# Experts' sums stored to their tokens' rows and read back in order; the last three experts added by products

## The chip, the core and the metric

The kernel runs on one core of one Trainium2 chip. The metric is the device time of one execution in microseconds (us). The core has a matrix engine (PE), a vector engine (VectorE, DVE), a scalar engine (ScalarE, ACT), GpSimd (POOL) and a queue that only issues transfers (SyncE, SP); 16 DMA engines carry the transfers of all queues. In the profile's DMA section q1 carries what SP issues, q10 what ScalarE issues, q0 what POOL issues.

## The reference

Two layers over 256 tokens `x` and 256 context tokens, each of width 1024. Layer 0 updates all 512 rows, layer 1 only the 256 of `x`. Each layer has a normalized, modulated attention and mixing part and then a mixture of 16 experts, of which each token uses two:

```python
h = rmsnorm(x, g) * (1 + scale) + shift
top2, weight = route(h)                    # grouped top-2 of 16 experts
for e in 16 experts:                       # d_model 1024 -> 512 -> 1024
    y[e] = (silu(h @ wg[e]) * (h @ wu[e])) @ wd[e]
x = x + gate * (weight[0] * y[top2[0]] + weight[1] * y[top2[1]])
out = rmsnorm(x, final_g)                  # after layer 1, rows of x only
```

All products of the experts are float32; each expert has 6 MB of weights a layer.

## The kernel before

**Slots.** An expert works on slots: 96 for the first `WIDE` experts of a layer (10 in layer 0, 6 in layer 1), 64 for the rest, which are taken in order of load. `g_route` writes a table `tab` of six numbers per token and expert (token number and weight, in pieces). A one-hot product with it gives each slot's token number `ids` and weight `csl`; an empty slot gets a number past the end, so its row is not gathered. `turn_tokens(e)` turns an expert's gathered rows for PE, `widen` makes the two projections, `inner` and `turn_inner` the gating, and `down` or `down_narrow` the third product and the scaled sums `yo`.

**Weights.** `Stream` (`W`) holds the list of all weight tiles in the order of use. `W.ahead()` issues loads on SP as far as free buffers and `W.limit` allow, several experts ahead. PE's order is written by hand; in the loop over `e` of `moe`, expert `e`'s projections stand between the parts of expert `e-1`.

**Sums and their way back.** `yo` of every expert goes, empty slots too, to `ybuf`, a buffer in DRAM laid out by expert and slot, by plain stores on ScalarE's queue (L1310, L1334). `rest()`, some 28 small VectorE instructions after expert 1, works out for each token the two rows `rowi` at which its sums stand. `combine_get` (L1182) gathers them by indirect loads on POOL, `combine` adds the two (L1190), multiplies by the gate in layer 0 (L1192) and adds to the token's row `xs` (L1194).

**The tail.** The last `TAIL` experts (two in layer 0, one in layer 1) reach the rows of `x` without DRAM: `others` keeps the scaled sums in `yx` (L1399), a product with a one-hot matrix `hotT` puts them at their tokens (`others_add`, L1366), and VectorE adds the product to `xs` (L1406). The gathers of the `x` rows are issued before the last expert's product in layer 0 and behind it in layer 1. Half of one tile's combine is done on POOL.

**After the experts.** In layer 0 the context's 256 rows are gathered (`yg`, `yh`), combined by VectorE and POOL, and normalized for layer 1; meanwhile two generators of projections (`uv0`, `uv1`) run, and two more (`ug`) beside the first half of the Hyena mixing (`g_hyf`). In layer 1 follow ScalarE's sums of squares (`junk`, L491), a square root with a table load (L493), VectorE's scaling (L2162) and the store of the output.

Of the kernel before, what the change touches and what calls it, by code (L numbers as in the profile page):

```python
# [36 lines left out]
TAIL = (2, 1)  # L37
# [212 lines left out]
def tile_hybrid_flow(ctx, tc, xin, rows, adab, w_ada, w_in_e, w_out_e, sinkb, rpb, w_in_o, w_out_o, hyw,  # L250
# [40 lines left out]
    def row_at(l, e):  # L291

        return min(e, WIDE[l]) * SLOTS[l] + max(e - WIDE[l], 0) * NARROW

    ybuf = [dram.tile([row_at(l, NE) + 1, D], F32, name=f"ybuf{l}") for l in range(2)]
# [30 lines left out]
    hyn = keep.tile([P, 8], F32, name="hyn")  # L326
    warm = keep.tile([P, 1], F32, name="warm")
# [629 lines left out]
    def slot_table(l, pool):  # L957

        NT = 4 if l == 0 else 2
        tab = pool.tile([P, NT, NE, 6], BF, name=f"tab{l}")  # L960
        tb3 = tok_b.rearrange("p (i a) -> p i a", a=2)[:, 0:NT]
        for a in range(2):
            G.tensor_copy(tab[:, :, :, a], tb3[:, :, a : a + 1].to_broadcast([P, NT, NE]))
        G.tensor_copy(tab[:, :, :, 2:3], cc("far").unsqueeze(1).unsqueeze(2).to_broadcast([P, NT, NE, 1]))
        return tab

    def g_route(l, pool, s, r):
# [78 lines left out]
        ids = kt("ids", [P, NE], I32)  # L1046
        csl = kt("csl", [P, NE])

        def find(src, n, idst, hp):
# [3 lines left out]
            newest["slots"] = V.tensor_scalar_add(idst, f, 4096.0).ins  # L1053

        def weigh(src, cdst):
            V.reduce_sum(cdst, src[:, :, 3:6], axis=AX.X)

        def slots(es, parts, idp=None):
            idp = tpt(f"ids{l}_{es[0]}")[:, 0] if idp is None else idp
            for e in es:  # L1060
                for i in range(NT):
                    hot = one_hot(pool, lambda i: posm[:, i * NE + e : i * NE + e + 1], 0, i, 4, e >= WIDE[l])
                    o = 6 * (e - es[0])
                    T.matmul(idp[:, o + parts.start : o + parts.stop], hot, tab[:, i, e, parts], start=(i == 0), stop=(i == NT - 1))
            return idp[:, 0 : 6 * len(es)].rearrange("p (e a) -> p e a", a=6)
# [37 lines left out]
        comb = rt("comb")  # L1103
# [15 lines left out]
        def group(e, idp):  # L1119

            idp = slots([e], slice(0, 6), idp)
            at = slice(e, e + 1)

            def rest():
                find(idp, 1, ids[:, at], pool)
                weigh(idp, csl[:, at])

            return rest

        def rest():  # L1130
            eb = kt("eb", [P, 2, NT])
# [9 lines left out]
            less = float(C - NARROW)  # L1141
            ri, late = kt("ri", [P, 2, NT]), kt("late", [P, 2, NT])
            V.scalar_tensor_tensor(ri, eb, float(SLOTS[l]), pq, op0=ALU.mult, op1=ALU.add)
            V.tensor_scalar(late, eb, float(-WIDE[l]), 0.0, op0=ALU.add, op1=ALU.max)
            V.scalar_tensor_tensor(ri, late, -less, ri, op0=ALU.mult, op1=ALU.add)
# [3 lines left out]
            rowi = keep.tile([P, 2 * NT], I32, name=f"rowi{l}")  # L1149
            zero = float(row_at(l, NE - TAIL[l]))  # L1150
            V.tensor_scalar(late, eb, NE - TAIL[l] - 0.5, None, op0=ALU.is_gt)
            V.scalar_tensor_tensor(ri, ri, -zero, late, op0=ALU.add, op1=ALU.add)
            V.tensor_mul(ri, ri, inm)
            V.tensor_scalar(late, late, -1.0, 1.0, op0=ALU.mult, op1=ALU.add)
            V.tensor_mul(ri[:, :, NT - 2 :], ri[:, :, NT - 2 :], late[:, :, NT - 2 :])
            V.tensor_scalar_add(rowi, ri.rearrange("p a i -> p (a i)"), zero)
            cmx = rt("cmx", [P, 1])
            top = rt("rtmp")[:, 0:NE]
            V.tensor_scalar(top, place, WIDE[l] - 0.5, less, op0=ALU.is_gt, op1=ALU.mult)
            V.tensor_add(top, top, pos[:, n16:])  # L1160
            V.reduce_max(cmx, top, axis=AX.X)
            cmi = kt("cmi", [P, 1], I32)
            V.tensor_copy(cmi, cmx)
            r.update(eb=eb, pq=pq, inm=inm, ri=ri, rowi=rowi, cmi=cmi)

        yield
        def weigh_first(idp):
            idp = slots([0, 1], slice(3, 6), idp)
            return lambda: weigh(idp, csl[:, 0:2])

        r.update(eids=eids, weigh_first=weigh_first, posm=posm, ids=ids, csl=csl, group=group, rest=rest, find=find, weigh=weigh, one_hot=one_hot, pos=pos)
# [6 lines left out]
    def combine_get(l, ys, src, rows_, i):  # L1178

        NT = 4 if l == 0 else 2  # L1180
        for a, t in enumerate(ys):
            newest["get"] = G.indirect_dma_start(out=t, out_offset=None, in_=src,  # L1182
                                                 in_offset=bass.IndirectOffsetOnAxis(ap=rows_[:, a * NT + i : a * NT + i + 1], axis=0)).ins
        return ys

# [10 lines left out]
    def moe(l, r, gate5):  # L1196
# [5 lines left out]
        posm, tab, ids, csl, one_hot, gts = (r[n] for n in ("posm", "tab", "ids", "csl", "one_hot", "gts"))  # L1202
# [75 lines left out]
        def turn_inner(e, he):  # L1278
# [5 lines left out]
            newest[S] = S.activation(hx[:, 0:2, 0:n], tp[:, 0:2, 0:n], AF.Copy).ins  # L1284
            newest[V] = V.tensor_copy(hx[:, 2:4, 0:n], tp[:, 2:4, 0:n]).ins
            return hx

        def down(e, hx):
# [21 lines left out]
            S.dma_start(yb[e * N : e * N + N, :], yo[0:N])  # L1310

        def down_narrow(e, hx):
# [22 lines left out]
            if l == 0 and e == NE - 1:  # L1335
                W.limit = until_moe0 + 1
                with tc.issue_after(d.ins):
                    W.ahead()
# [3 lines left out]
        def others_slots():  # L1342

            t = W.pools["extra"][0].tile([P, 2, D], F32, name=f"hotT{l}", tag="wt")[:, 0, 0 : 2 * TAIL[l] * P].rearrange("p (n t) -> p n t", t=P)
            tp = tpt(f"hotp{l}")
# [859 lines left out]
```

## Time and profile before

| | |
|---|---|
| median of 3 runs | 1160.65 us (1160.2 to 1163.1) |
| the profiled execution | 1164.05 us |
| its span, first to last instruction | 1162.2 us |
| busy: PE, VectorE, ScalarE, POOL | 1002.1, 557.4, 380.5, 166.0 us |
| moved by DMA | 329.40 MB |
| mean clock granted to PE | 0.94 |

The profiled execution took 1.85 us more than its span and 3.40 us more than the median. Times in the trace count from the first instruction. PE is busy for 86% of the span; the rest is to be looked for stage by stage.

### The profile page before, as it was taken

Reading aid. Unit: us, or ns where it says so; the run is one execution under the profiler, and the core shown is the slowest. Engines: PE = TensorE matmul, PEld = TensorE weight load, DVE = VectorE, ACT = ScalarE, POOL = GpSimd, SP = SyncE. Lnnn points to the kernel's source line nnn. Section 1 sums busy time; section 2 is a strip of 40 time slices with the busy share of each in tenths; the row PEclk is TensorE's granted clock in tenths of the full one; section 3 lists DMA queues with packets and bytes.
Section 4 is the critical chain, followed back from the end, with each engine's and each line's share of the span. In section 5 each row is a group of like instructions: output and inputs, shape, how many; then the busy total and the mean of one; then the engine's idle time right before and its main releaser. Section 6 shows DMA issues by size and latency. Waiting matters only on the chain. (4 is left out here: it accounts for less than half of the span.)

```text
span 1162.2 us, 20926 instructions
## 1 busy us (share of the span) xinstructions
PE 1002.1 (86%) x8390; PEld 554.8 (48%) x8390; DVE 557.4 (48%) x1390; ACT 380.5 (33%) x852; POOL 166.0 (14%) x184
## 2 busy tenths in 40 slices
PE   5899999889893899999998479978884999998881
PEld 2477877557672333333332367766661333332220
DVE  5665555567547533433312874566765533321113
ACT  2554453332322233333221452443341322211111
POOL 2320001210205000000001621312012000000002
PEclk9999999999896899999999789989996999999996
DMA  8931121892967999999999656435297899999993
GB/s 319 417 117 73 73 73 46 297 330 76 393 264 267 312 310 390 403 392 396 403 397 406 252 230 231 154 142 207 73 401 283 278 370 406 408 390 418 418 410 114
DMA packets 56014, 329.40 MB, mean 283 GB/s; under 512 B 8611, under 2 KB 9091, under 8 KB 21795
## 3 DMA queue, kind: packets, MB, share of 16 engines
q1 hardware_dynamic: 40195, 278.85, 61.5%
q0 software_dynamic: 10960, 35.99, 9.3%
q10 hardware_dynamic: 4752, 13.12, 3.2%
q8 instruction: 69, 1.13, 0.4%
q14 instruction: 38, 0.30, 0.1%
HBM read 315.54 MB, written 16.58 MB: 286 GB/s over the span
## 5 line engine op out<-in xcount | busy, mean ns | idle before, releaser
L1234 PE MATMUL gu<-wt,tx 128*32 128x512 f32 x2560 | 305.5, 606 | 12.9 <-DMA wt<-in_moe_wu_dram 10.6
L1234 PEld LDWEIGHTS gu<-wt,tx 128*32 128x32 f32 x2560 | 82.7, 111 | 203.2 <-issue 169.8
L1234 PE MATMUL y<-wt,hx 128*32 128x512 f32 x1280 | 147.5, 593 | 2.4 <-DMA wt<-in_moe_wd_dram 1.5
L1234 PEld LDWEIGHTS y<-wt,hx 128*32 128x32 f32 x1280 | 43.1, 110 | 97.1 <-issue 92.2
L515 DVE TENSOR_TENSOR pair<-wt,pair 128x512 fp32r<-128x512 f32 x104 | 68.8, 711 | 18.5 <-ACT pair L512 18.3
L1223 ACT ACTIVATE tx<-gp 128x192 f32<-128x192 f32 (+1 forms) x64 | 19.3, 304 | 154.7 <-PE gp L1214 119.8
L1265 DVE TENSOR_TENSOR yo<-yo,y 32x512 f32<-32x512 f32 x32 | 21.8, 683 | 90.9 <-ACT yo L1263 90.6
L512 ACT ACTIVATE pair<-wt 128x512 fp32r<-128x512 f32 x104 | 58.4, 626 | 15.6 <-DMA wt<-in_w_in_o_dram 14.5
L1224 DVE COPY tx<-gp 128x192 f32<-128x192 f32 (+1 forms) x64 | 20.3, 322 | 81.5 <-ACT tx L1223 81.0
L1275 DVE TENSOR_TENSOR he<-he,up 96x512 f32<-96x512 f32 (+1 forms) x32 | 21.9, 685 | 72.1 <-ACT up L1274 71.5
L429 PE MATMUL ada<-wt,siluT 128*32 128x128 f32 x1536 | 52.4, 287 | 2.8 <-ACT pt L770 2.0
L1270 ACT ACTIVATE he<-gu 96x512 f32<-96x512 f32 (+1 forms) x32 | 18.9, 591 | 98.8 <-PE gu L1234 98.8
L429 PEld LDWEIGHTS ada<-wt,siluT 128*32 128x32 f32 x1536 | 42.2, 114 | 14.2 <-issue 7.1
L954 POOL DMA_INDIRECT gt<-h2d,ids x16 | 15.5, 972 | 204.5 <-DVE hot L1176 92.2
L954 POOL DMA_INDIRECT rows<-h2d,ids x16 | 15.3, 958 | 185.2 <-DVE hot L1176 95.0
L1265 DVE TENSOR_TENSOR up<-up,gu 32x512 f32<-32x512 f32 x32 | 21.8, 683 | 38.0 <-ACT up L1263 37.7
L768 PE MATMUL tp<-ident,pr 128*128 128x128 f32 x256 | 33.9, 275 | 0.0
L757 DVE TENSOR_SCALAR pr<-pr,ls 128x512 f32<-128x512 f32 (+1 forms) x80 | 32.5, 457 | 1.1
L741 ACT ACTIVATE pr<-sB,ng 128x512 f32<-128x512 f32 (+1 forms) x32 | 18.2, 578 | 41.9 <-DVE ng L734 36.2
L768 PEld LDWEIGHTS tp<-ident,pr 128*128 128x128 f32 x256 | 28.7, 141 | 4.5 <-issue 1.6
L520 PE MATMUL op<-pair,oh 128*128 128x512 f32 x64 | 27.1, 424 | 3.2 <-DVE pair L515 3.1
L519 PE MATMUL op<-pair,ol 128*128 128x512 f32 x64 | 27.7, 433 | 1.7 <-ACT pair L512 1.7
(500 smaller groups left out, 1923.8 us busy)
## 6 DMA issues: line engine op xcount, KB each, us to landing
wt<-in_moe_wg_dram SPq DMA_DIRECT2D x63, 1024.0 KB
wt<-in_moe_wd_dram SPq DMA_DIRECT2D x63, 1024.0 KB
wt<-in_moe_wu_dram SPq DMA_DIRECT2D x62, 1024.0 KB
wt<-in_w_ada_dram SPq DMA_DIRECT2D x45, 1024.0 KB
wt<-in_w_in_e_dram SPq DMA_DIRECT2D x9, 1024.0 KB
ybuf<-yo ACTq DMA_DIRECT2D x16, 384.0 KB
wt<-in_w_in_o_dram SPq DMA_DIRECT2D x5, 1024.0 KB
bc<-mrow POOLq DMA_DIRECT2D x9, 512.0 KB, 10.1
```

The lines of the kernel that those rows point to most:

```text
L429: T.matmul(ps[32 * j : 32 * j + 32, 0:P], siluT[:, k, :], w[:, k % 4, 128 * j : 128 * j + 128], start=(k == 0), stop=(k == KD - 1), tile_p ...
L512: newest["whi"] = S.activation(hi, w, AF.Copy).ins
L515: newest[eng] = eng.tensor_sub(lo, w, hi.bitcast(F32)).ins
L519: T.matmul(o, al, bh, start=first, stop=False)
L520: T.matmul(o, ah, bl, start=False, stop=False)
L757: V.tensor_scalar_mul(pr[:, h, at], pr[:, h, at], ls[:, h, j : j + 1])
L768: T.transpose(tp[:, kc], pr[:, h, kc * P : kc * P + P], ident)
L954: return G.indirect_dma_start(out=dst, out_offset=None, in_=h2d[l], in_offset=bass.IndirectOffsetOnAxis(ap=idx, axis=0), bounds_check=h2d[ ...
L1224: V.tensor_copy(tx[:, q * 4 + 2 : q * 4 + 4, 0:n], tp[:, 2:4, 0:n])
L1234: T.matmul(o[32 * c : 32 * c + 32], lhs, rhs, start=first, stop=last, tile_position=(0, 32 * c))
L1265: V.tensor_add(dst[q : q + 32], dst[q : q + 32], b[q : q + 32])
L1275: V.tensor_mul(he[0:n], he[0:n], up[0:n])
```

## The change

`ybuf` is now laid out by token: two rows for each. `tab` gets a seventh number that tells whether an expert is a token's first or second, and `aim` makes each slot's target row `tgt` from it. `scatter` stores `yo` by an indirect transfer on POOL's queue that skips empty slots; each waits for the one before to land. Since a token's row may not be written when its expert's sum is added by a product or lies past its slots, `ybuf` is first filled with zeros by four transfers from one 1 KB tile (`zero_rows`), 6 MB in pieces of 1 KB. A plain load of 1 MB (`combine_load`) brings 128 tokens' pairs of rows. `TAIL` is three in both layers. `rest()` moves into the branch for overflowing experts; five instructions, `most()`, stay. The last expert's `hx` is copied by ScalarE alone, POOL combines nothing any more, `others_take` runs before the last expert's sums, and layer 1's first weights are issued by SP during expert 15. Behind layer 0 four generators (`u0` to `u3`) stand beside the context's combine. A square root's table is brought in early at the end.

```diff
-TAIL = (2, 1)
+TAIL = (3, 3)
...
-    ybuf = [dram.tile([row_at(l, NE) + 1, D], F32, name=f"ybuf{l}") for l in range(2)]
+    ybuf = [dram.tile([2 * TT, D], F32, name=f"ybuf{l}") for l, TT in enumerate((512, 256))]
...
+        which = rt("sel")
+        V.tensor_scalar(which[:, 0:NE], base, -1.0, 16.0, op0=ALU.mult, op1=ALU.add)
...
+        V.tensor_scalar(which_of, posm, 0.5, None, op0=ALU.is_gt)
+        V.tensor_tensor(i3(which_of), i3(which_of), which[:, 0:NE].unsqueeze(1).to_broadcast([P, NT, NE]), op=ALU.mult)
+        V.reduce_max(first_of, i3(which_of), axis=AX.X)
+        V.tensor_tensor(tab[:, :, :, 6], i3(which_of), first_of.unsqueeze(2).to_broadcast([P, NT, NE]), op=ALU.is_lt)
...
+    def combine_load(l, t, i):
+
+        G.dma_start(t, ybuf[l][2 * P * i : 2 * P * (i + 1)].rearrange("(p a) d -> p a d", a=2))
+        return [t[:, a] for a in range(2)]
...
+        def scatter(dst, src, idx):
+
+            G.indirect_dma_start(out=dst, out_offset=bass.IndirectOffsetOnAxis(ap=idx, axis=0), in_=src, in_offset=None,
+                                 bounds_check=dst.shape[0] - 1, oob_is_err=False)
...
-            S.dma_start(yb[e * N : e * N + N, :], yo[0:N])
+            scatter(yb, yo[0:N], tgt[0:N, e : e + 1])
...
-            row = row_at(l, e) + last
-            for b in range(2):
-                d = (SY if e == NE - 1 else S).dma_start(yb[row : row + NARROW, 512 * b : 512 * b + 512], yo[NARROW * b : NARROW * b + NARROW])
...
+            rows_ = yb[0 : (TT if last else 2 * TT)].rearrange("r (b n) -> (r b) n", b=2)
+            scatter(rows_, yo, tgt[:, e : e + 1])
...
+        def others_take(i):
+
+            with tc.issue_after(newest["yx"]):
+                combine(l, gate5, NT - 2 + i, ex["rows", i])
...
-            else:
-                others_rows()
-                others_open()
+            if e in (NE - 2, NE - 1):
+                others_rows(NE - 1 - e)
...
+            if e == NE:
+                for i in (1, 0):
+                    others_take(i)
+                others_open()
...
+            if e == NE - 1:
+                W.limit = len(specs)
...
+        def zero_rows(l, half):
+
+            n = ybuf[l].shape[0] // 2
+            t = ybuf[l][half * n : half * n + n].rearrange("(p r) (b n) -> p (r b) n", p=P, b=4)
+            SY.dma_start(t, zero.to_broadcast([P, t.shape[1], 256]))
+            yield
...
+        fill = chain(ada_row(0), gate_rows(), zero_rows(0, 0), ada_row(1), reload(), zero_rows(0, 1), ada_row(2), ahead_first(), zero_rows(1, 0), first_out(),
+                     ada_row(3), zero_rows(1, 1), ada_row(4), ada_row(5), ahead_out())
...
-                combine(0, gate5, i, ys[i], (V, G)[i])
+                combine(0, gate5, i, ys[i], adds=False)
+                yield
+                combine(0, gate5, i, ys[i], sums=False)
...
-        dense = chain(*[g_fm(sp, hh, hl, 256, ev_u(2 * j), f"uv{j}") for j in range(2)])
+        dense = chain(*[g_fm(sp, hh, hl, 256, ev_u(2 * j), f"u{j}") for j in range(4)])
```

Before the change VectorE's rows at the end of layer 1's experts read as follows (`he` gating, `yo` and `yx` scaled sums, `rows` and `yr` gathered pairs, `last` the one-hot products):

```order
L1275 TENSOR_TENSOR he_15_10480<-he_15_10480,up_15_10481 64x512
L1331 SCALAR_TENSOR_TENSOR yo_14_10476<-y_14_10459,csl_8467,gate5x_8562 128x512
L1285 COPY hx_15_10499<-hp_15_10494 128x2x64
L1399 SCALAR_TENSOR_TENSOR yx_10522<-y_15_10502,csl_8467,gate5x_8562 128x512
L1190 TENSOR_TENSOR rows_8241<-rows_8241 128x1024
L1194 TENSOR_TENSOR xs_1909<-xs_1909,rows_8241 128x1024
L1406 TENSOR_TENSOR xs_1909<-xs_1909,last_00_10490 128x512
L1406 TENSOR_TENSOR xs_1909<-xs_1909,last_10_10492 128x512
L1190 TENSOR_TENSOR rows_8241<-rows_8241,yr_10485 128x512
L1406 TENSOR_TENSOR xs_1909<-xs_1909,last_01_10491 128x512
L1194 TENSOR_TENSOR xs_1909<-xs_1909,rows_8241 128x512
L1406 TENSOR_TENSOR xs_1909<-xs_1909,last_11_10493 128x512
```

With the change the same engine has there (`yr` is the pair read back for each of two tiles):

```order
L1302 TENSOR_TENSOR he_15_10623<-he_15_10623,up_15_10624 64x512
L1413 SCALAR_TENSOR_TENSOR yx_10553<-y_14_10605,csl_8551,gate5x_8654 128x512
L1212 TENSOR_TENSOR yr_10472<-yr_10472 128x1024
L1216 TENSOR_TENSOR xs_1911<-xs_1911,yr_10472 128x1024
L1212 TENSOR_TENSOR yr_10577<-yr_10577 128x1024
L1216 TENSOR_TENSOR xs_1911<-xs_1911,yr_10577 128x1024
L1413 SCALAR_TENSOR_TENSOR yx_10553<-y_15_10651,csl_8551,gate5x_8654 128x512
L1419 TENSOR_TENSOR xs_1911<-xs_1911,last_00_10639 128x512
L1419 TENSOR_TENSOR xs_1911<-xs_1911,last_10_10641 128x512
L1419 TENSOR_TENSOR xs_1911<-xs_1911,last_01_10640 128x512
L1419 TENSOR_TENSOR xs_1911<-xs_1911,last_11_10642 128x512
```

The sums of the pairs moved from behind the last `yx` to ahead of it, and behind it four additions of products are left.

POOL's queue around the end of layer 0's experts reads, before (the gathers of `x` rows, POOL's half of a combine, the branch for overflow, the context's gathers, layer 1's first weights):

```order
L1182 DMA gt_0_3109<-ybuf_75,rowi_3966 128x1024
L1182 DMA gt_1_3110<-ybuf_75,rowi_3966 128x1024
L1182 DMA yr_5780<-ybuf_75,rowi_3966 128x1024 x2
L1190 TENSOR_TENSOR yr_5780<-yr_5780 128x512
L1192 TENSOR_TENSOR yr_5780<-yr_5780,bc_5_3440 128x512
L1194 TENSOR_TENSOR xs_1909<-xs_1909,yr_5780 128x512
L1450 TENSOR_LOAD cmi_3978
```

And with the change (each scatter to `ybuf` waits for the one before it):

```order
L1232 DMA ybuf_75<-yo_12_5661,tgt_3518 2048x512
L1205 DMA yr_5688<-ybuf_75 128x2048
L1232 DMA ybuf_75<-yo_13_5771,tgt_3518 1024x512
L1205 DMA yr_5798<-ybuf_75 128x2048
L1232 DMA ybuf_75<-yo_14_5842,tgt_3518 1024x512
L1232 DMA ybuf_75<-yo_15_5917,tgt_3518 1024x512
L1468 TENSOR_LOAD cmi_3981
```

Both loads of the `x` rows now stand ahead of expert 15's scatter; they need the scatter of expert 12. The last three scatters of layer 0 write rows of the context alone.

On SP the fill is issued among the weights of the first layer's B attention; before:

```order
L230 DMA wt<-in_w_ada_dram 128x2048 x12
L230 DMA wt<-in_w_out_e_dram 128x2048 x2
L1801 DMA xs_1908<-in_xin_dram 128x1024 x2
L1801 DMA xs_1909<-in_xin_dram 128x1024 x2
L230 DMA wt<-in_w_ada_dram 128x2048 x12
```

with the change:

```order
L230 DMA wt<-in_w_ada_dram 128x2048 x10
L1855 DMA ybuf_75<-zero 2048x1x256
L230 DMA wt<-in_w_ada_dram 128x2048 x2
L230 DMA wt<-in_w_out_e_dram 128x2048 x2
L1821 DMA xs_1910<-in_xin_dram 128x1024 x2
L1821 DMA xs_1911<-in_xin_dram 128x1024 x2
L1855 DMA ybuf_75<-zero 2048x1x256
L230 DMA wt<-in_w_ada_dram 128x2048 x5
L1855 DMA ybuf_76<-zero 1024x1x256
L230 DMA wt<-in_w_ada_dram 128x2048 x5
L1855 DMA ybuf_76<-zero 1024x1x256
```

The first fill stands ahead of the last two `w_ada` tiles of that run and of `w_out_e`, the second behind the `xs` rows, the last two among the next `w_ada` tiles.

## Rows read from the trace of the kernel before

**Rows 1.** The page: the span, and busy time of each engine.

```profile
span 1162.2 us, 20926 instructions
PE 1002.1 (86%) x8390; PEld 554.8 (48%) x8390; DVE 557.4 (48%) x1390; ACT 380.5 (33%) x852; POOL 166.0 (14%) x184
```

**Rows 2.** Stretches: length, busy time by engine, PEclk, DMA share, GB/s.

```profile
200.00:220.00 20.00, 18.22 (x237) 11.81 (x234) 12.41 (x32) 6.28 (x19) 6.74 (x10) 1.00 0.71 201
220.00:264.00 44.00, 37.38 (x384) 24.58 (x382) 27.43 (x70) 16.58 (x51) 8.82 (x14) 1.00 1.00 347
264.00:300.00 36.00, 34.62 (x337) 25.21 (x339) 24.86 (x55) 10.71 (x33) 0.71 (x2) 1.00 0.36 131
340.00:360.00 20.00, 16.89 (x92) 11.92 (x90) 13.48 (x25) 9.66 (x20) 10.30 (x4) 0.87 0.20 52
640.00:680.00 40.00, 20.27 (x107) 17.37 (x108) 34.67 (x43) 19.20 (x37) 24.96 (x21) 0.70 0.77 293
```

**Rows 3.** Timeline of PE around the layers' ends; in brackets idle time, releaser.

```profile
651.11 0.45 PE L536 MATMUL xt<-ident,xn 128*128 128x128 f32 x1 [8.31 <-ACT xn L491]
...
673.37 0.55 PE L519 MATMUL uv<-hh,pair 128*128 128x256 f32 x1 [8.32 <-DVE rsn L494]
...
1133.98 1.92 PE L1234 MATMUL y<-wt,hx 128*32 128x512 f32 x16 [0.57 <-DMA wt<-in_moe_wd_dram]
1136.77 1.99 PE L1366 MATMUL last<-yx,hotT 64*128 64x512 f32 x8 [0.86 <-DVE yx L1399]
```

**Rows 4.** Timeline of VectorE at the end of layer 1.

```profile
1135.96 0.75 DVE L1399 SCALAR_TENSOR_TENSOR yx<-y,csl,gate5x 128x512 f32<-128x512 f32 x1 [4.82 <-PE y L1234]
1143.58 1.22 DVE L1190 TENSOR_TENSOR rows<-rows 128x1024 f32<-128x1024 f32 x1 [6.87 <-DMA rows<-ybuf,rowi]
...
1150.60 0.69 DVE L1406 TENSOR_TENSOR xs<-xs,last 128x512 f32<-128x512 f32 x1
```

**Rows 5.** Timeline of ScalarE at the end of layer 1.

```profile
1151.71 1.06 ACT L491 ACTIVATE junk<-xs 128x1024 f32<-128x1024 f32 x1 [20.89 <-DVEq L1452]
...
1153.91 1.28 ACT L493 ACT_TABLE_LOAD   x1
```

**Rows 6.** Timeline of VectorE at the end of layer 0.

```profile
632.83 0.75 DVE L1399 SCALAR_TENSOR_TENSOR yx<-y,csl,gate5x 128x512 f32<-128x512 f32 x1 [1.08 <-PE y L1234]
...
637.14 1.22 DVE L1190 TENSOR_TENSOR gt<-gt,gt 128x1024 f32<-128x1024 f32 x1 [0.57 <-DMA yr<-ybuf,rowi]
...
640.00 0.75 DVE L1399 SCALAR_TENSOR_TENSOR yx<-y,csl,gate5x 128x512 f32<-128x512 f32 x1 [0.38 <-PE y L1234]
...
646.84 1.27 DVE L1406 TENSOR_TENSOR xs<-xs,last 128x512 f32<-128x512 f32 x2
...
661.16 3.37 DVE L1190 TENSOR_TENSOR yg<-yg,yh 128x1024 f32<-128x1024 f32 x1
```

**Rows 7.** Timeline of POOL after layer 0.

```profile
660.84 2.60 POOL L1190 TENSOR_TENSOR yg<-yg,yh 128x1024 f32<-128x1024 f32 x1 [3.21 <-DMA yh<-ybuf,rowi]
```

**Rows 8.** Timeline of VectorE and PE in the route of layer 0.

```profile
387.99 0.20 DVE L1114 CAST cb<-comb 128x64 bf16<-128x64 f32 x1
...
388.55 0.24 PE L1064 MATMUL gp<-tab,hot 128*128 128x3 bf16 x4 [0.47 <-DVE tab L1115]
```

**Rows 9.** DMA queues in 203:206 and in 620:624: packets, MB, share.

```profile
q0 software_dynamic: 228, 0.60, 100.4%
...
q10 hardware_dynamic: 160, 0.26, 17.3%
```

**Rows 10.** Timeline of ScalarE and SP in the first layer's B attention.

```profile
221.31 8.41 SPq L230 DMA_DIRECT2D wt<-in_w_out_e_dram  x2
...
244.33 1.70 ACT L512 ACTIVATE pair<-wt 128x512 fp32r<-128x512 f32 x3
```

**Rows 11.** Waits of the issuing queue SP.

```profile
SPq L230 <- DMA ybuf<-yo: 78.3, 16, 9.4
```

**Rows 12.** Waits of PE for the second projection's weights.

```profile
PE gu L1234 <- DMA wt<-in_moe_wu_dram: 10.6, 8, 2.2
```

More of the change, by code (lines that the diff above doesn't have):

```diff
@@ L959, in slot_table @@
         NT = 4 if l == 0 else 2
-        tab = pool.tile([P, NT, NE, 6], BF, name=f"tab{l}")
+        tab = pool.tile([P, NT, NE, 7], BF, name=f"tab{l}")
         tb3 = tok_b.rearrange("p (i a) -> p i a", a=2)[:, 0:NT]
@@ L1119, in group, with most @@
         def group(e, idp):
-            idp = slots([e], slice(0, 6), idp)
+            idp = slots([e], slice(0, 7), idp)
             at = slice(e, e + 1)
             def rest():
-                find(idp, 1, ids[:, at], pool)
+                f = find(idp, 1, ids[:, at], pool)
                 weigh(idp, csl[:, at])
+                aim(idp, f, 1, tgt[:, at], e >= WIDE[l])
             return rest
+        less = float(C - NARROW)
+        def most():
+            cmx = rt("cmx", [P, 1])
+            top = rt("rtmp")[:, 0:NE]
+            V.tensor_scalar(top, place, WIDE[l] - 0.5, less, op0=ALU.is_gt, op1=ALU.mult)
+            V.tensor_add(top, top, pos[:, n16:])
+            V.reduce_max(cmx, top, axis=AX.X)
+            cmi = kt("cmi", [P, 1], I32)
+            V.tensor_copy(cmi, cmx)
+            r.update(cmi=cmi)
         def rest():
@@ L1148, in rest @@
             V.tensor_scalar(inm, pq, C - 0.5, None, op0=ALU.is_lt)
[L1149 to L1164, printed above, removed]
+            return eb, pq, inm, ri
         yield
         def weigh_first(idp):
-            idp = slots([0, 1], slice(3, 6), idp)
-            return lambda: weigh(idp, csl[:, 0:2])
-        r.update(eids=eids, weigh_first=weigh_first, posm=posm, ids=ids, csl=csl, group=group, rest=rest, find=find, weigh=weigh, one_hot=one_hot, pos=pos)
+            idp = slots([0, 1], slice(0, 7), idp)
+            def rest():
+                weigh(idp, csl[:, 0:2])
+                aim(idp, find(idp, 2, ids[:, 0:2], pool), 2, tgt[:, 0:2], False)
+            return rest
+        r.update(eids=eids, weigh_first=weigh_first, posm=posm, ids=ids, csl=csl, group=group, rest=rest, most=most, tgt=tgt, find=find, weigh=weigh, one_hot=one_hot, pos=pos)
         yield
@@ L1348, in others_slots, with others_rows @@
                 j = (NT - 2 + n % 2) * NE + NE - 1 - n // 2
                 slots_hot(hot, posm[:, j : j + 1])
-                T.transpose(tp[:, n], hot, ident)
-            S.activation(t, tp[:, 0 : 2 * TAIL[l]], AF.Copy)
+                T.transpose(tp[:, n % 4], hot, ident)
+                if n % 4 == m - 1:
+                    S.activation(t[:, n - m + 1 : n + 1], tp[:, 0:m], AF.Copy)
             ex["hot"] = t
-        def others_rows():
-            if l == 0:
-                t = W.pools["extra"][0].tile([P, 2, D], F32, name="yr0", tag="wt")
-                d = [gts[0], gts[1], t[:, 0], t[:, 1]]
-            else:
-                d = [gts[0], gts[1], r["third"], keep.tile([P, 2, D], F32, name="yr1", tag="xr0")[:, 0]]
-            ex["rows"] = [combine_get(l, d[2 * i : 2 * i + 2], yb[0 : row_at(l, NE - TAIL[l]) + 1, :], r["rowi"], NT - 2 + i) for i in range(2)]
-            return newest["get"]
+        def others_rows(i):
+            if i and l:
+                t = keep.tile([P, 2, D], F32, name="yr1", tag="xr0")
+            else:
+                t = W.pools["rest" if i else "more"][0].tile([P, 2, D], F32, name=f"yr{l}{i}", tag="wt")
+            ex["rows", i] = combine_load(l, t, NT - 2 + i)
@@ L1826, in gate_rows @@
             yield
-        fill = chain(ada_row(0), gate_rows(), ada_row(1), reload(), ada_row(2), ahead_first(), first_out(), ada_row(3), ada_row(4), ada_row(5), ahead_out())
+        zero = pe.tile([P, 1, 256], F32, name="zero")
+        G.memset(zero, 0.0)
+        def zero_rows(l, half):
[5 more added lines that the diff above has]
+                     ada_row(3), zero_rows(1, 1), ada_row(4), ada_row(5), ahead_out())
         weave(g_attend(pq, [chunk_b(c) for c in range(4)]), fill, 1.26)
@@ L1918, in tile_hybrid_flow @@
             get(i)
-        W.limit = len(specs)
-        W.ahead(G)
+        W.ahead()
         for i in (2, 3):
```

95 lines of the change are left out of this document (44 added, 51 removed).

## The prediction

> **What bounds the kernel now.** I read the page first, then the stretches by stage, then the timelines at the ends of the two layers. The page gives PE 1002.1 us of a span of 1162.2 [rows 1], so at most 160 us can be had without taking work from PE. Those 160 us are not spread evenly. In the stretches two places stand out: in 640 to 680 PE is busy for only 20.27 of 40 us, at a granted clock of 0.70 [rows 2], and behind 1138.76 (1136.77 + 1.99, PE's last row) PE does nothing more until the span ends at 1162.2 [rows 3, 1]. Both lie behind the experts, where the change works.
>
> At the end of layer 1 the chain runs so. VectorE scales the last expert's sums at 1135.96, then waits 6.87 us for the gathered rows, and combines until 1150.60 + 0.69 = 1151.3 [rows 4]. ScalarE has been idle for 20.89 us when it begins its sums of squares at 1151.71, and a table load of 1.28 us stands ahead of the square root [rows 5]. From the last expert's `yx` to `junk` it is 15.75 us, and nothing covers it.
>
> At the end of layer 0 `yx` of expert 15 stands at 640.00 and the last addition ends at 646.84 + 1.27 = 648.1 [rows 6]. PE waits 8.31 us for ScalarE's normalized rows (to 651.11), and again 8.32 us (to 673.37) for the context's [rows 3]. Before the second wait VectorE takes the context's rows as its combine: the first add at 661.16 took 3.37 us [rows 6], while POOL did the same addition on its half, from 660.84 on [rows 7]. The same operation took 1.22 us at 637.14, when POOL did no such work [rows 6].
>
> **(a) The end of layer 1.** The two additions for each of two tiles (1.22 us each at 1143.58 [rows 4], so 4.9) now stand between the `yx` of expert 14 and that of expert 15. The last product's expert takes longer than that, with two more experts' products (1.99 us for each, the row at 1136.77 [rows 3]) ahead of it on PE. If the plain loads have landed, what is left from the start of the last `yx` on is 0.75 for itself, 1.0 for the half of the product that the first tile needs, and four additions of 0.69 [rows 4]: 4.5 us. Before it was 1151.3 - 1135.96 = 15.3. ScalarE so begins 10.8 us earlier, and the table load of 1.28 leaves the chain, since ScalarE is idle for 20.89 us there [rows 5] and can bring the table in ahead. Together -12. Bounds: -15 if the last pieces overlap better, -7 if the read-back is late by one combine of 4.9.
>
> **(b) The end of layer 0.** The combine is three operations for a tile, 1.22 each [rows 6], 7.3 us for both, all on VectorE and all ahead of the last `yx`. `yx` of expert 14 ended at 632.83 + 0.75 = 633.6, 6.4 us before that of expert 15 [rows 6], and PE gets 1.99 us more of products in between. So the combine nearly fits, and the last `yx` comes 1.5 to 2 us later. Behind it 0.75 + 1.0 + four additions of 0.68 are 4.5 us, against 8.1 before. I take -2.5 (-5 if PE's extra products hide in other waits, 0 if the combine begins late).
>
> **(c) The head of layer 1.** Four projections stand where two stood, and the other two are no longer needed later, so PE's second wait of 8.32 us [rows 3] has work in it. The context's combine on VectorE alone is six operations at 1.22, 7.3 us, against some 10 for three at 3.37 [rows 6]: not longer, if it is POOL's work that made them 3.3. The first weights come from SP during expert 15 and not behind the gathers. Some of the clock of 0.70 [rows 2] comes back as PE stands still less. I take -9: the wait, and 1 for the clock. Bounds -13 (all that and 5 us of the clock) and -4 (the context is later and half the wait comes back).
>
> **(d) The route.** Five small instructions on VectorE stand ahead of the last entries of `tab`, for which PE waits 0.47 us [rows 8]. They are of 128x32 to 128x64, and the cast of 128x64 beside them takes 0.20 us [rows 8]. In layer 0 that is 1.0, in layer 1 0.5 to 0.8: +1.5 (0.5 to 2.5). The 28 small instructions that go stood off the path, so they give nothing.
>
> **(e) The zeros.** 6 MB go out in 6144 pieces of 1 KB, and no row shows such pieces. The bounds are the two nearest: the experts' sums in 2 KB pieces, 160 packets at 17.3% of 4 us of 16 engines, 69 ns each; and POOL's mixed small loads, 228 packets at 100.4% of 3 us, 211 ns each [rows 9]. That is 26 or 81 us of all engines. The DMA engines are idle for 0.29 of 20 us, 0.64 of 36 and 0.80 of 20 between 200 and 360 [rows 2]: 5.8 + 23.0 + 16 = 44.8 us, which holds pieces of up to 117 ns. I take a price near the first, since those too are stores from a tile to DRAM. Even so the first 2 MB stand on SP ahead of `w_out_e`, issued from 221.31 and used at 244.33 [rows 10], in a stretch where the engines are full [rows 2]: 2048 pieces at 69 ns put them off by 9 us, of which I let 3 come through. So +3 (0 to 8).
>
> The Trainium skill (DMA: Bandwidth & Descriptors, Specifications) says that transfers of at least 512 bytes run at line rate, so 1 KB pieces would cost by bytes: by 2 KB pieces at 69 ns they would be 35 ns each, 13 us in all, and the term nothing. The row at 211 ns, with 2.6 KB to a packet on the mean (0.60 MB by 228), does not agree.
>
> **(f) The experts' transfers and products.** In layer 1 the stores were 6 x 96 + 9 x 64 = 1152 rows of 4 KB, 4.7 MB; now at most 512, 2.1 MB, and the read-back adds 2.1 MB ahead of the last weights. In layer 0 it is 1344 rows (5.5 MB) against at most 1024 (4.2 MB), and 2.1 MB more. At the 347 GB/s of a full stretch [rows 2] that is -1.5 us and +2.3 us of transfers. SP waited 78.3 us for the stores' landings [rows 11], a wait that goes away, but PE waited for weights only 10.6 us in 8 places [rows 12]. PE gains two experts' products and four transposes in layer 1, some of it in place of such waits, like the 0.57 us at 1133.98 [rows 3]. I take +1.5 (-6 to +5).
>
> The sum is -12 - 2.5 - 9 + 1.5 + 3 + 1.5 = -17.5. The profiled execution took 1164.05 us (its span and 1.85 around it), so 1146.5; it stands 3.4 above the median, so the median becomes 1143.
>
> **The rivals.** *The read-back is late.* Each 1 MB load waits for the scatter of expert 12 and shares the engines with the weights. VectorE's combine stands ahead of the last `yx` in order; when its pair isn't there, expert 15's sums wait too, and PE's last products behind them. A lane's landing took up to 9.4 us [rows 11]. Late by a combine at both ends (5 us each), and with the context's rows 2 late behind the last scatter, it is -17.5 + 12 = -5.5: 1155. For it speaks that scatter 12 and two loads now follow each other within two experts. Against it, that two experts are over 20 us.
> The Trainium skill (DMA: Bandwidth & Descriptors, Two DMAs through the same engine are not ordered) says that only a transfer's completion tells that its bytes have landed, so a load must wait for the store's landing. By that, this chain of scatter, landing, issue and load can't be shortened; gathers waited the same way before, 6.87 us on VectorE [rows 4].
>
> *The experts become faster.* If what held PE was the lanes of the stores (78.3 us of SP's waits [rows 11]), the 10.6 us of waits for weights go [rows 12]: 1132.
>
> *The zeros cost.* This ends on the other side. At 211 ns a piece 81 us of transfers meet 44.8 idle ones, and the experts' first weights wait the 36 us that are left: -17.5 - 3 + 36 = +15.5, 1176. It decides from 117 ns on, and the change loses from about 170 ns (20.5 us more than the idle time: 65.3 x 16 / 6144). Against it stands that the pieces at 211 ns are POOL's gathers of strided rows, not stores.
>
> *It evens out.* Late read-backs and zeros at their upper bound of 8 together leave nothing: within 3.5 us of 1160.
>
> **How the numbers follow.** The forecast 0.56, read-backs late 0.17, faster experts 0.14, costly zeros 0.07, evened out 0.06. Faster by over 0.3% (3.5 us, about what can be told from no change here) are the first three: 0.87; same 0.06; slower 0.07. The range reaches from the faster experts to the late read-backs, 1130 to 1156, and leaves out the last two.
>
> **What would show it.** (a) `junk` begins about 5 us behind the last product and no table load follows it. (b) the last addition to `x` rows comes 4.5 us behind PE's end. (c) PE has no wait of 8 us for the context, and VectorE's adds there take 1.2 us. (e) the fill's packets take 40 to 100 ns, and `w_out_e` is waited for by a few us. (f) PE's waits for weights stay near 10 us. Wrong would be a wait of VectorE for `yr` ahead of the last `yx`, experts that take longer because gathers wait on POOL behind scatters, or a DMA stretch that is full through 264 to 300 and on to 360.

## The result and the profile after

The changed kernel took 1168.95 us in the median of 6 runs (1163.97 to 1173.71), the kernel before beside it 1159.43 (1157.57 to 1163.1, 6 runs): a ratio of 1.008, 95% interval 1.0055 to 1.0105. It is slower by 0.8%, where 1143 was forecast. The profiled execution took 1173.71 us, 1.8 more than its span. The page's first lines, against [rows 1]:

```profile
span 1171.9 us, 21017 instructions
PE 1015.3 (87%) x8420; PEld 561.7 (48%) x8420; DVE 557.8 (48%) x1429; ACT 382.4 (33%) x855; POOL 165.0 (14%) x192
```

The sum hides large changes of both signs. To place them I cut both traces at the same rows of PE: the first turned tokens of layer 0's experts (`gp<-ident,gt`), the last one-hot product of expert 15 (`last`, the row that waits for `yx`), the first turned row of layer 1 (`xt`), its first turned key (`kvct`), the first turned tokens of layer 1's experts (`gp<-ident,rows`), its last `last`, and the span's end. The differences of these starting times, in us, each from one profiled execution:

| stretch | before | after | difference | forecast |
|---|---|---|---|---|
| start to experts of layer 0 | 380.43 | 395.93 | +15.5 | (e) +3 |
| experts of layer 0, route's end included | 260.38 | 266.04 | +5.7 | (d), (f) |
| `last` to `xt` | 10.30 | 7.08 | -3.2 | (b) -2.5 |
| `xt` to `kvct` | 80.45 | 80.29 | -0.2 | (c) -9 |
| `kvct` to experts of layer 1 | 160.45 | 160.44 | 0.0 | (d) |
| experts of layer 1 | 244.76 | 248.82 | +4.1 | (f) |
| `last` to the end | 25.43 | 13.30 | -12.1 | (a) -12 |
| span | 1162.2 | 1171.9 | +9.7 | -17.5 |

(d) and (f) together were forecast at +3 and came to +9.8, with nothing of it in the last route. How far such a stretch differs between executions shows in the changed kernel and the first four runs below, whose code is the same in the experts and behind them but for one edit in the head of layer 1: experts of layer 0 264.04 to 266.04, experts of layer 1 248.60 to 249.09, and without that edit `xt` to `kvct` 79.82 to 80.92.

**The largest loss lies where the zeros are issued.** PE's timeline behind the B attention, whose last product (`oB`) is the first row, before:

```profile
307.54 1.08 PE L782 MATMUL oB<-pt,vB 128*64 128x256 f32 x8
308.55 1.95 PE L429 MATMUL ada<-wt,siluT 128*32 128x128 f32 x64
...
310.69 1.08 PE L429 MATMUL ada<-wt,siluT 128*32 128x128 f32 x32
```

and with the change:

```profile
313.74 1.08 PE L779 MATMUL oB<-pt,vB 128*64 128x256 f32 x8
314.75 4.57 PE L426 MATMUL ada<-wt,siluT 128*32 128x128 f32 x160
322.65 2.13 PE L426 MATMUL ada<-wt,siluT 128*32 128x128 f32 x32 [3.32 <-DMA wt<-in_w_ada_dram]
...
325.42 1.93 PE L426 MATMUL ada<-wt,siluT 128*32 128x128 f32 x32 [0.24 <-DMA wt<-in_w_ada_dram]
...
331.22 0.47 PE L414 MATMUL adat<-ident,ab 128*128 128x128 f32 x1 [3.24 <-DVE mod L415]
```

Before, three tiles of modulation products (`ada`, 32 products each) stood behind the last `oB`; now it is seven (160 + 32 + 32 products), and two wait for weights. These two took 2.13 and 1.93 us in place of 1.08: the granted clock is 0.50 (1.2 GHz) in their stretches, after 1.00 (2.4 GHz) in 310 to 318; in between PE stood idle for the weights. SP issues the second half of `w_out_e` behind these tiles' weights, 15 us later than before (its queue, before and after):

```profile
300.75 1.20 SPq L230 DMA_DIRECT2D wt<-in_w_out_e_dram  x2
```

```profile
315.89 1.20 SPq L230 DMA_DIRECT2D wt<-in_w_out_e_dram  x2
```

ScalarE's first split of it (a split makes a `pair` of fp32r tiles, high and low part, from a float32 weight tile, with VectorE's help), without a wait before, now waits 13.28 us (ScalarE's timeline, before and after):

```profile
308.95 1.66 ACT L512 ACTIVATE pair<-wt 128x512 fp32r<-128x512 f32 x3
```

```profile
328.53 1.67 ACT L509 ACTIVATE pair<-wt 128x512 fp32r<-128x512 f32 x3 [13.28 <-DMA wt<-in_w_out_e_dram]
```

PE's timeline around the layers' ends, against [rows 3]:

```profile
638.36 5.32 PE L1261 MATMUL gu<-wt,tx 128*32 128x512 f32 x28 [1.44 <-DMA wt<-in_moe_wu_dram]
...
661.97 1.99 PE L1393 MATMUL last<-yx,hotT 64*128 64x512 f32 x8 [1.38 <-DVE yx L1413]
669.05 0.45 PE L533 MATMUL xt<-ident,xn 128*128 128x128 f32 x1 [5.09 <-ACT rsn L490]
...
687.65 0.36 PE L516 MATMUL u<-hh,pair 128*128 128x256 f32 x1 [2.21 <-DVE uc L1932]
...
692.72 0.39 PE L516 MATMUL u<-hh,pair 128*128 128x256 f32 x1 [3.41 <-DVE pair L512]
...
730.15 0.79 PE L516 MATMUL kvck<-hh,pair 128*128 128x512 f32 x1 [5.71 <-DVE ab L431]
...
1137.01 5.33 PE L1261 MATMUL gu<-wt,tx 128*32 128x512 f32 x28 [3.92 <-DMA wt<-in_moe_wu_dram]
...
1158.60 1.99 PE L1393 MATMUL last<-yx,hotT 64*128 64x512 f32 x8 [0.87 <-DVE yx L1413]
```

The wait for normalized rows is 5.09 in place of 8.31. The wait of 8.32 for the context is gone, but waits of 2.21, 3.41 and 5.71 stand behind it. At 1137.01 PE waits 3.92 us for the last expert's second projection; before, the longest such wait was 2.2 [rows 12] and this one 1.44:

```profile
1116.98 3.63 PE L1234 MATMUL gu<-wt,tx 128*32 128x512 f32 x28 [1.44 <-DMA wt<-in_moe_wu_dram]
```

The same 28 products took 5.33 us where they took 3.63 before: behind the longer wait the mean granted clock is 0.68, before it was 1.00. In layer 0 of this profile it is the same (5.32 us at 0.68, behind waits of 0.97 and 1.44).

VectorE's timeline, against [rows 4] and [rows 6]:

```profile
681.77 1.23 DVE L1212 TENSOR_TENSOR yg<-yg 128x1024 f32<-128x1024 f32 x1 [1.40 <-DMA yg<-ybuf]
...
1150.32 0.75 DVE L1413 SCALAR_TENSOR_TENSOR yx<-y,csl,gate5x 128x512 f32<-128x512 f32 x1 [1.51 <-PE y L1261]
1150.99 1.22 DVE L1212 TENSOR_TENSOR yr<-yr 128x1024 f32<-128x1024 f32 x1
...
1154.63 1.22 DVE L1216 TENSOR_TENSOR xs<-xs,yr 128x1024 f32<-128x1024 f32 x1
1157.79 0.75 DVE L1413 SCALAR_TENSOR_TENSOR yx<-y,csl,gate5x 128x512 f32<-128x512 f32 x1 [1.93 <-PE y L1261]
...
1159.76 2.48 DVE L1419 TENSOR_TENSOR xs<-xs,last 128x512 f32<-128x512 f32 x4 [1.21 <-PE last L1393]
```

The context's first addition takes 1.23 us, not 3.37. At the end of layer 1 the pairs' sums follow the `yx` of expert 14 without a wait, so the read-back was there in time, and end before the last `yx`. In layer 0 the six operations of the combine end just as the last `yx` starts, and PE waits 1.38 us for it where it waited 0.87. ScalarE's timeline there, against [rows 5]:

```profile
1151.59 1.28 ACT L2192 ACT_TABLE_LOAD   x1 [0.51 <-ACTq L1470]
...
1162.58 1.06 ACT L488 ACTIVATE junk<-xs 128x1024 f32<-128x1024 f32 x1
```

The table load stands 11 us ahead of `junk`, and `junk` begins 4.8 us after the last `yx` began; before it was 15.75. In the route of layer 0 PE's wait for `tab` grew from 0.47 [rows 8] to 2.37, and counted from the first turned tokens the product came 1.35 us later (9.47 in place of 8.12):

```profile
405.40 0.24 PE L1073 MATMUL gp<-tab,hot 128*128 128x7 bf16 x4 [2.37 <-DVE tab L1132]
```

### The profile page after: what moved, and what is told of

Read it like the earlier page. It is cut to its first block, busy times and chain, and to the rows that moved or that the text cites. A ratio compares the mean times of both kernels' runs of the same rounds, so it can differ in the third digit from the quotient of the medians.

```text
span 1171.9 us, 21017 instructions
## 1 busy us (share of the span) xinstructions
PE 1015.3 (87%) x8420; PEld 561.7 (48%) x8420; DVE 557.8 (48%) x1429; ACT 382.4 (33%) x855; POOL 165.0 (14%) x192
## 5 line engine op out<-in xcount | busy, mean ns | idle before, releaser
L1261 PE MATMUL gu<-wt,tx 128*32 128x512 f32 x2560 | 305.6, 610 | 15.2 <-DMA wt<-in_moe_wu_dram 11.2
L1232 POOL DMA_INDIRECT ybuf<-yo,tgt x29 | 28.1, 970 | 275.0 <-DVE yo L1337 103.1
```

The lines of the kernel that those rows point to most:

```text
L1232: G.indirect_dma_start(out=dst, out_offset=bass.IndirectOffsetOnAxis(ap=idx, axis=0), in_=src, in_offset=None, bounds_check=dst.shape[0] - ...
L1261: T.matmul(o[32 * c : 32 * c + 32], lhs, rhs, start=first, stop=last, tile_position=(0, 32 * c))
```

## The experiments

Ratios are to the kernel before, run beside each group on the same chip (medians 1158.72, 1157.07, 1157.43 and 1159.12 us), with 95% intervals. Single executions of one kernel spread over up to 1.3%, so effects are read from ratios, and within a profile from stretches, not from one end time. Where two ratios' intervals leave their difference open, the text says so.

### The zeros: steps or transfers?

`weave` takes 1.26 steps of the side work (`fill`) for each step of the attention and runs what is left of it behind the attention. Each `zero_rows` is such a step, though PE has nothing to do in it.

Zeros ahead of the first layer's A attention, no steps:

```diff
...
+        for l in range(2):
+            n = ybuf[l].shape[0] // 2
+            for half in range(2):
...
+                SY.dma_start(t, zero.to_broadcast([P, t.shape[1], 256]))
         weave(g_attend(pq, [chunk_a(c) for c in range(4)]), dense, .97)
...
```

> The four fills with zeros are issued on SP before the first layer's A attention, where the DMA engines are mostly idle, and no steps for them stand among the work beside the B attention. In the changed kernel PE reaches the experts of layer 0 15.5 us later than before. Both theories expect most of this back: about 1155 us, 14 less than the changed kernel's 1169, and PE's first turned tokens of layer 0 within 3 us of the 380.43 us of before. If it stays above 1164, the zeros are not the cause.

1158.37 us, ratio 0.9999 (0.9973 to 1.0024). Layer 0's experts begin at 381.37, and three tiles stand behind the last `oB` again (PE's timeline):

```profile
306.96 1.08 PE L779 MATMUL oB<-pt,vB 128*64 128x256 f32 x8
307.98 1.96 PE L426 MATMUL ada<-wt,siluT 128*32 128x128 f32 x64
...
310.12 1.08 PE L426 MATMUL ada<-wt,siluT 128*32 128x128 f32 x32
```

All that the changed kernel lost against the one before is back, and no more: the gains and the other losses cancel.

Zeros early, but four empty steps left in the side work:

```diff
...
-            SY.dma_start(t, zero.to_broadcast([P, t.shape[1], 256]))
+        def step():
             yield
...
```

> Fills early as in the run before, but four empty steps are left where the fills stood among the work beside the B attention, so PE's order is that of the changed kernel and the transfers are not. Theory 1 (each fill is a step of the interleaving, so four steps of the side work fall behind the attention, uncovered): 1166 to 1170 us, and the layer's experts begin 14 us late. Theory 2 (the 6 MB of transfers delay weights in a full stretch): 1154 to 1157 us.

1168.45 us, ratio 1.008 (1.005 to 1.0109); the experts begin at 395.74. Without one byte of zeros in that stretch ScalarE waits for `w_out_e` again (its timeline):

```profile
326.03 1.67 ACT L509 ACTIVATE pair<-wt 128x512 fp32r<-128x512 f32 x3 [9.33 <-DMA wt<-in_w_out_e_dram]
```

Zeros at their places, without steps of their own:

```diff
             SY.dma_start(t, zero.to_broadcast([P, t.shape[1], 256]))
-            yield
...
+            yield from then
```

> The fills are issued at their places beside the B attention, but each together with the step that follows it, so the interleaving has no steps more than before. Theory 1 (the steps): 1154 to 1158 us. Theory 2 (the transfers): 1166 to 1170 us. Something between the two means that both have a part.

1158.59 us, ratio 0.9996 (0.9977 to 1.0015); the experts begin at 382.59. In 264 to 300 the DMA share is 0.65 (before, 0.36 [rows 2]), and PE's busy time is what it was, 34.6 us:

```profile
264.00:300.00 36.00, 34.63 (x320) 25.21 (x318) 25.30 (x56) 10.96 (x32) 0.55 (x1) 1.00 0.65 251
```

The transfers do show: ScalarE waits 4.00 us for the second half of `w_out_e`, where it waits 0.65 with the zeros early.

```profile
314.58 1.67 ACT L509 ACTIVATE pair<-wt 128x512 fp32r<-128x512 f32 x3 [4.00 <-DMA wt<-in_w_out_e_dram]
```

But little or nothing of it reaches the experts: they begin 1.2 us later than with the zeros early, less than that start differs among the profiles of kernels with early zeros and no steps (378.36 to 386.45). So theory 1 (the steps) is shown: within what can be told, the four steps cost the whole of it.

### The bias rows of layer 1

In the changed kernel POOL loads the bias rows for layer 1's modulation behind two of its additions for the Hyena mixing (POOL's timeline):

```profile
720.96 2.52 POOL L2076 TENSOR_TENSOR K<-K,zt 128x512 f32<-128x512 f32 x2 [3.12 <-DVE K L2075]
723.41 1.64 POOL L401 DMA_DIRECT2D ab<-in_adab_dram  x3
```

```diff
+    held[0] = ada_bias(*order_c[0][0:2], po)
     weave(g_hyf(0, Ks[0]), chain(dense, ada_row(0)), 1.2)
```

> The changed kernel with one edit: the bias rows for layer 1's first modulation row are loaded ahead of the first half of the Hyena mixing, not behind two of POOL's additions in it. In the changed kernel PE waits 5.71 us for them (before the change 0.3). If that wait is on the path: 1163 to 1165 us, 4 to 6 below the changed kernel. If a later wait takes its place: 1168 to 1170.

1169.14 us, ratio 1.0082 (1.0052 to 1.0112), no gain that could be told. Before the change the load stood behind the same two additions (at 701.66); what changed is that PE has less work left to do until it needs the rows. In the profile the wait of 5.71 us is gone and `xt` to `kvct` is 77.30 in place of 80.29; a wait of PE for ScalarE has come in behind it:

```profile
739.06 0.70 PE L516 MATMUL kvcv<-hh,pair 128*128 128x512 f32 x1 [3.10 <-ACT rawk L2012]
```

### The experts: products or read-back?

All four have the zeros early, without steps (ratio 0.9999). Expert 13's and 14's products left out:

```diff
...
-            for e in range(NE - TAIL[l], NE - 1):
-                for i in range(2):
-                    others_add(e, i)
```

> Base: the kernel with the zeros issued early (1158.4 us). Here the products of experts 13 and 14 with their one-hot matrices are left out (the sums of the last expert alone are added to the rows of x by products), in both layers. They are 4 us of PE's work ahead of the last expert's third product. If that work sets when the last expert ends: 1150 to 1153 us, 3 to 4 less in each layer. If the weights' arrival sets it: 1157 to 1159.

1153.48 us, ratio 0.9968 (0.9937 to 0.9999), whose difference to the base's 0.9999 (0.9973 to 1.0024) is not clear of noise. The experts' stretches shrink by 0.9 us in layer 0 (265.25 to 264.32), which is within the spread of that stretch, and by 2.3 in layer 1 (248.71 to 246.41), which is not.

Read-back cut to a sixteenth:

```diff
-            ex["rows", i] = combine_load(l, t, NT - 2 + i)
+            G.memset(t[:, :, 64:], 0.0)
+            G.dma_start(t[:, :, 0:64], yb[n : n + 2 * P, 0:64].rearrange("(p a) d -> p a d", a=2))
```

> Same base. The read-back of the pairs for the rows of x brings 64 of 1024 columns, so 15/16 of the experts' sums of those rows are left out; the other columns are set to zero by POOL. If the two loads of 1 MB delay the weights that PE waits for (3.4 us for the last expert's second projection in layer 1, against 1.4 before the change): 1149 to 1153 us, 3 to 5 less in each layer. If not: 1157 to 1159.

1146.06 us, ratio 0.9915 (0.9878 to 0.9953): 0.84% less, 9.7 us. The experts' stretches are 259.25 and 244.42, 6.0 and 4.3 us less. The wait in question in layer 1, on PE's timeline of the base kernel:

```profile
1121.99 5.04 PE L1261 MATMUL gu<-wt,tx 128*32 128x512 f32 x28 [3.42 <-DMA wt<-in_moe_wu_dram]
```

and all of PE's waits for second projections without read-back (total, times, longest), 10.1 in 6 places in the base and 10.6 in 8 before [rows 12]:

```profile
PE gu L1261 <- DMA wt<-in_moe_wu_dram: 5.6, 5, 1.4
```

Scatters and gathers keep their order on POOL in this run, and its experts take what they took before the change (260.38 and 244.76). So gathers that wait on POOL behind scatters, one of the prediction's signs of being wrong, are not what made the experts longer.

Expert 13's products ahead of expert 15's projections, and the bias early:

```diff
...
+            if e == NE - 1:
+                others_open()
+                others_early(NE - 3)
...
```

> Same base, with two edits and all of the computation: expert 13's products stand ahead of expert 15's first projections, where PE waits for weights, and layer 1's bias rows are loaded ahead of the Hyena mixing. If products cost where they stand: 2 us less in each layer, and the bias up to 5: 1150 to 1154. If the loads and the splits set the pace anyway: 1156 to 1159.

1152.79 us, ratio 0.9976 (0.9954 to 0.9998): 2.7 us less in the ratio, which is not clear of noise either. The experts' stretches fall by 0.9 us (within the spread) and 1.6 us.

The last scatter of layer 0 left out:

```diff
-            if l and last:
+            if last and (l or e == NE - 1):
                 return
```

> Same base. The last expert's sums for the context rows of layer 0 are not stored, so the read-back of the context waits for the scatter of expert 14 and not for that of expert 15, which itself waits for it; expert 15's sums are left out of the context rows. If the chain of scatters sets when the context's rows are there and these set the head of layer 1: 1150 to 1153 us. If VectorE's and ScalarE's splits of weights set it: 1156 to 1159.

1155.75 us, ratio 0.9995 (0.9971 to 1.002): nothing that can be told in the time, though `xt` to `kvct` is 77.12 against 80.38 in the base's profile, more than the spread above. The chain of scatters is at most a part of it.

### The read-back behind the weights

```diff
-            ex["rows", i] = combine_load(l, t, NT - 2 + i)
+            ex["rows", i] = combine_load(l, t, NT - 2 + i, SY)
...
-            if e in (NE - 2, NE - 1):
-                others_rows(NE - 1 - e)
+            if e == NE - 1:
+                for i in (1, 0):
+                    others_rows(i)
```

> Base: the kernel with the zeros issued early (1158.4 us), all of the computation. The two loads that read the pairs of the rows of x back are issued on SP behind the layer's last weights and no longer on POOL among them. If their 2 MB cost by standing ahead of weights that PE waits for: most of the 9.8 us per run without read-back comes back, 1149 to 1153 us, and PE's wait for the last expert's second projection in layer 1 falls from 3.4 to under 2 us. If the loads then land too late, VectorE's sums of the pairs hold up the last expert's sums: 1156 to 1161.

1153.82 us, ratio 0.9951 (0.9925 to 0.9977): 5.6 us less, over half of what leaving the loads out had brought. The experts' stretches are 262.53 and 244.79, 2.7 and 3.9 us less, and 0.9 to 1.0 of that goes again behind `last` in each layer (7.96 and 14.50, against 7.09 and 13.46). The same with expert 13's products moved and the bias early:

> The same, with expert 13's products ahead of expert 15's projections and layer 1's bias rows loaded early (together 2.4 us less in the ratio, measured on the base). If the parts add: 1146 to 1151 us, ratio to the kernel before 0.990 to 0.994. If the wait for weights that hid expert 13's products is gone with the loads' new place: 1150 to 1154.

1148.65 us, ratio 0.9916 (0.9885 to 0.9947), faster than both kernels. The stretches are 258.95 and 244.47. On PE's timeline at the end of layer 1 the wait for the second projection is gone, and expert 13's products stand ahead of it:

```profile
1115.51 1.99 PE L1393 MATMUL last<-yx,hotT 64*128 64x512 f32 x8 [0.96 <-DVE yx L1414]
1117.43 2.78 PE L1261 MATMUL gu<-wt,tx 128*32 128x512 f32 x24
...
1135.77 1.99 PE L1393 MATMUL last<-yx,hotT 64*128 64x512 f32 x8 [0.87 <-DVE yx L1414]
```

The price is on VectorE, which waits for a pair and adds the rest behind the last `yx`:

```profile
1132.47 1.22 DVE L1212 TENSOR_TENSOR yr<-yr 128x1024 f32<-128x1024 f32 x1 [3.19 <-DMA yr<-ybuf]
1134.96 0.75 DVE L1414 SCALAR_TENSOR_TENSOR yx<-y,csl,gate5x 128x512 f32<-128x512 f32 x1 [1.27 <-PE y L1261]
1135.63 1.22 DVE L1216 TENSOR_TENSOR xs<-xs,yr 128x1024 f32<-128x1024 f32 x1
```

So the stretches behind `last` are 11.50 us in layer 0 and 15.23 in layer 1, against 7.09 and 13.46 with early zeros alone. Net of that the two layers' experts give 1.9 and 2.5 us. `xt` to `kvct` is 74.74 against 80.38, but it also begins 4.4 us later behind `last`: from `last` to `kvct` 1.2 us are left (86.24 against 87.47), and the runs don't tell which of the edits gave how much of the 5.6. That this kernel is faster than the one with the loads alone moved (0.9951) is likely and not shown; the intervals overlap.

### The head of layer 1

Both have this last kernel as base (0.9916). In the first run the context's combine is left out; the second has its second tile on POOL:

```diff
-                combine(0, gate5, i, ys[i], adds=False)
+                combine(0, gate5, i, ys[i], (V, G)[i], adds=False)
                 yield
-                combine(0, gate5, i, ys[i], sums=False)
+                combine(0, gate5, i, ys[i], (V, G)[i], sums=False)
```

> Base: the kernel with read-back behind the weights, early products and early bias (1148.7 us). The six operations on VectorE that combine the context's rows behind layer 0 are left out, so the experts' sums don't reach the context's rows; loads and everything else stay. If these operations, in VectorE's order ahead of the splits of weights and the convolutions that PE waits for (3.4 us twice), are what took the place of the 8.3 us wait: 1140 to 1144 us. If something else sets the head of layer 1: 1147 to 1150.

1146.53 us, ratio 0.9894 (0.984 to 0.9949): the interval holds the base's ratio, so the time does not decide. The profile does for the stretch: `xt` to `kvct` is 67.83 against 74.74, and PE's longest wait for a split there is 0.88 where it was 3.42. The row in the base, and the one in its place:

```profile
679.29 0.58 PE L516 MATMUL u<-hh,pair 128*128 128x256 f32 x1 [3.42 <-DVE pair L512]
```

```profile
667.40 0.39 PE L516 MATMUL u<-hh,pair 128*128 128x256 f32 x1 [0.88 <-DVE pair L512]
```

> Same base, all of the computation. The second context tile is combined by POOL, beside VectorE's first, as before the change. If the operations take 3.3 us again when both engines run (before: 3.37, alone 1.22), VectorE is held as long or longer than by six operations at 1.22: 1148 to 1152 us. If only the amount of VectorE's work counts: 1144 to 1147.

1148.31 us, ratio 0.9934 (0.9899 to 0.997), the same as the base; `xt` to `kvct` is 74.65 against 74.74. POOL's three operations took 2.4 to 2.7 us each, and VectorE's work beside them slowed down, the splits of two tiles from 1.28 us together to 4.06 (POOL's timeline, then VectorE's):

```profile
665.22 2.38 POOL L1212 TENSOR_TENSOR yg<-yg 128x1024 f32<-128x1024 f32 x1 [14.64 <-DMA yg<-ybuf]
667.69 2.68 POOL L1214 TENSOR_TENSOR yg<-yg,bc 128x1024 f32<-128x1024 f32 x1
670.45 2.70 POOL L1216 TENSOR_TENSOR xs<-xs,yg 128x1024 f32<-128x1024 f32 x1
```

```profile
666.86 4.06 DVE L512 TENSOR_TENSOR pair<-wt,pair 128x512 fp32r<-128x512 f32 x2
```

## Why the prediction was wrong

**(e) failed, and with it the sign.** The step that failed is "the first 2 MB stand on SP ahead of `w_out_e` [...] put them off by 9 us, of which I let 3 come through". I costed the zeros as transfers. As transfers they cost nothing that can be told (0.9996 with all of them in place; of the delay of `w_out_e`, 4.00 us at ScalarE, 1.2 at most reached the experts). What cost +15.5 us was a term that I had put at nothing without seeing it: the four steps in an interleaving that has a fixed ratio (1.008 with the steps alone). Four tiles of modulation work then fall behind the attention, where nothing covers them, and what follows them in order (the second half of `w_out_e`, issued as their buffers come free) is late as well. The order of PE before and after shows it without any run; I read it on VectorE, POOL and SP and not there. The rival of costly zeros (0.07) had the right sign for the wrong reason: it priced a piece at 211 ns, and that its sum of +15.5 for the whole kernel is also the loss of this one stretch is chance. The packets behind those 211 ns are plain loads of `E` and `ab` on POOL's queue, not gathers as the prediction says.

**(f) failed in its size, by where the bytes stand.** The balance of bytes was right: scatters save about what the read-back adds (by rate and length the experts of layer 0 moved 100.0 MB where they had moved 98.9, those of layer 1 91.8 and 92.5). But the saving is spread over the stage, while the 2 MB come just ahead of the last expert's projections. Without them the experts of the two layers take 6.0 and 4.3 us less; behind the weights they cost a little under half as much (4.1 us of 9.7 by the ratios). Not all of the 6.0 and 4.3 us is waiting: PE's busy time for the same instructions falls by 3.2 and 1.6 us without the loads (255.71 to 252.49, 236.42 to 234.82), so products ran slower with them, as the 28 behind the wait in layer 1 do. The prediction had no such term. The products of experts 13 and 14 cost 2.3 us in layer 1; in layer 0, where those of expert 14 stood before too, no cost can be told. The late read-back rival named the loads but not the loser: VectorE found its pairs in time, PE did not find its weights. The rival of faster experts fell: SP no longer waits for the stores' landings (78.3 us [rows 11]), and PE's waits for second projections are 11.2 us in place of 10.6.

**(c) failed.** Of 9 us forecast 0.2 came, and of the clock nothing: the mean granted in `xt` to `kvct` is 0.85, before 0.87. The operations did go back to 1.23 us, and PE did have projections in the old wait. But the projections need splits and convolutions from VectorE, which now stand behind six operations of the combine in its order; in the last kernel leaving these out shortens the stretch by 6.9 us, though no gain in the time could be told. And with the two generators moved up, PE came to POOL's bias load, behind its additions as before, with nothing left to cover it: 5.71 us, of which 3.0 came back with the load early. The old wait was cut in pieces and not filled.

**(a), (b) and (d) held.** The end of layer 1 gave 12.1 us for 12 forecast. That of layer 0 gave 3.2 behind `last`; (b) had 3.6 there and took off 1.5 to 2 for a late last `yx`, and of that some 0.5 shows (PE's wait of 1.38 for 0.87), so its -2.5 is right to within a us. PE's wait in the route grew by 1.9 us in layer 0 and by nothing in layer 1, for 1.5 together. VectorE's pairs fit between the two `yx`, as worked out.

With the steps gone, the read-back behind the weights, one expert's products moved and the bias early, the change does gain: 0.9916 against 1.008. What is left open is how much of (c) can be had: context sums elsewhere than on VectorE or POOL were not tried.

## What to carry to other kernels

Where work is interleaved by a count of steps, a new item costs a step even when it issues one transfer; attach it to a step that is there, and compare the matrix engine's own order at the end of the stretch. Bytes saved early in a stage that is bound by transfers did not pay here for bytes added ahead of its last loads: put a read-back behind the last weight in the same queue. A wait that is to be filled with other work needs that work's own inputs: look which engine makes them, and what was put ahead of them on it.

## What the runs showed of the hardware

Stores of zeros in pieces of 1 KB run as fast as weights. In the run with the zeros early next to nothing else moves in 106 to 116, and the DMA queues' lines there are:

```profile
DMA packets 3787, 3.87 MB, mean 387 GB/s; under 512 B 21, under 2 KB 3786, under 8 KB 3786
...
q1 hardware_dynamic: 3786, 3.86, 108.4%
```

108.4% of 10 us of 16 engines by 3786 packets are 46 ns a piece, and 387 GB/s is what the experts' transfers reach too (380 in layer 0 before). So the price of 69 ns taken for a zero was too high and 211 far off. The Trainium skill (DMA: Bandwidth & Descriptors, Specifications) puts the bound for line rate at 512 bytes; this trace agrees for pieces of 1 KB.

A wait of PE can cost more than its length: behind three of them the granted clock is lower. In the changed kernel 32 `ada` products took 2.13 us at 0.50 behind a wait of 3.32 (1.08 at 1.00), 28 projections 5.33 at 0.68 behind 3.92 (3.63 at 1.00 before), and behind the 5.71 us at `kvck` the granted clock is 0.57 up to 735 and 1.00 from there to 738.

VectorE slows down beside POOL whoever does the combine: beside POOL's operations its split of two tiles took 4.06 us (1.28 without them), as its addition took 3.37 before (1.22). That fits that half the work on POOL brought nothing.
